# The small work of a state space group in three portions instead of seven

## The chip, the core and the metric

The kernel runs on one core of a Trainium2 chip. The metric is the device time of one execution in microseconds (us). A core has five engines that run side by side and wait for each other by semaphores: TensorE (PE, matrix products; the profile shows its weight loads apart, as PEld), VectorE (DVE), ScalarE (ACT), GpSimd (POOL) and SyncE (SP), which here issues the transfers between the chip's memory (HBM) and the core's own memory. Products are accumulated in eight PSUM banks of 128 x 512 floats.

## The reference, cut to what matters

One block of a hybrid model on 512 positions with width 1024: a norm, one wide projection, a state space branch and an attention branch that are gated and added, then a feed-forward part. Attention has nothing to do with the change except that its last step, the combination of three attention groups, runs on DVE at the same time. The state space branch is this:

```python
def ssd_chunked(xs, dt, A, Bm, Cm):
    ...                                   # G = 8 groups, K = 4 heads each, N = 128, Q = 128, 4 chunks
    X = (xs * dt[..., None]).reshape(b, c, Q, G, K, P)
    a_cs = jnp.cumsum(a, axis=-1)
    Ldec = jnp.exp(jnp.where(causal, seg, -jnp.inf))          # seg = a_cs_l - a_cs_s
    CB = jnp.einsum('bclgn,bcsgn->bcgls', Cc, Bc)
    y_diag = jnp.einsum('bcgkls,bcsgkp->bclgkp', CB[:, :, :, None] * Ldec, X)
    states = jnp.einsum('bclgn,bcgkl,bclgkp->bcgkpn', Bc, decay_states, X)
    ...                                   # prev: the states carried from chunk to chunk
    y_off = jnp.einsum('bclgn,bcgkpn,bcgkl->bclgkp', Cc, prev, jnp.exp(a_cs))
    return (y_diag + y_off).reshape(b, s, H, P)

def ssd_branch(z, xbc, dt_raw, conv_w, conv_b, dt_bias, a_log, d_skip, norm_g):
    xbc = jax.nn.silu(causal_dwconv(xbc, conv_w, conv_b))
    xs, Bm, Cm = jnp.split(xbc, (D_INNER, D_INNER + SSD_GROUPS * D_STATE), axis=-1)
    ...
    y = ssd_chunked(xs, dt, A, Bm, Cm) + d_skip.astype(f32)[:, None] * xs
    y = y.reshape(b, s, D_INNER) * jax.nn.silu(z.astype(f32))
    y = rms_norm(y.reshape(b, s, SSD_GROUPS, SSD_NORM_GROUP), norm_g.reshape(SSD_GROUPS, SSD_NORM_GROUP))
```

## The kernel before

**Pieces.** All weights come in pieces of 512 KB. SP loads a piece into `raw` (three buffers), ACT rounds it to `whi` (L103) and DVE subtracts to get the rest, `wlo` (L104); each of these has three buffers too, and one is free again when the last product that reads it is through. A channel piece is 24 products of 128 x 512 into one bank of four (tag "mm"): eight with whi and the high part of the activations (`hh,whi`), eight with the low part (`hl,whi`), eight with `hh,wlo` (`mm_chan`, L143).

**Ticks.** Small work hangs on this stream. It is written as generators; `tick()` lets each of them go on by one step when its wait, counted in ticks, is over. Ticks fall after product 12 of a piece, where `prefetch` also sets the next split going, and at the end of a piece. PE runs its instructions exactly in the order in which they are written, so a step's matmuls stand where its tick stands. For DVE, ACT, POOL and SP the scheduler chooses the order.

**A group of the state space stage** has six pieces: B and C (tile `bct`), two of xs (`xst`), two of z (`zs`). ACT and DVE run the convolution from PSUM (L676, L52), ACT the silu (L798). `ssd_side(g)` is the small work. `bc` holds the decays, copied to all partitions by SP (L688); DVE subtracts (L704), ACT takes relu (L706) and exp (L707). Then PE's portions, with the banks' tags:

- cb and bt (L713, L719): the products of C and B, and transposes of B, in the middle of a piece; DVE masks cb (L714) and multiplies it into bc (L722)
- xt, twice (L732): transposes of `xst`, at a piece's end and in the middle of the next; DVE makes `xdt` and `xdc` from each (L735, L738)
- st (L744): the chunk states from `xdc` and `btok`, in the two banks of tag "aux"; DVE carries them on as `prev` (L749 to L753)
- y with o (L763, L768), twice: y reads `bc` and `xdt`, o reads `bct` and `prev`; DVE and ACT go on from there (L771 to L774)
- n (L784): the norm's sum, from `sr` (ACT L780, POOL L777 and L781)

That is seven portions a group. [...] `load_decay(g + 2)` issues the next bc into the buffer that y1 has released. Two numbers set the waits between a group's portions for normal groups (`GN`), and others for the first two groups (`G0`, `G1`), the third (`G2W`), the norm (`NL`) and attention's combination (`COMB`), whose products and sums on DVE are L644, L646 and L652.

Of the kernel before, what the change touches and what calls it, by code (L numbers as in the profile page):

```python
# [16 lines left out]
P = 128  # L17
S = 512
NT = S // P
# [4 lines left out]

LAG, PVLAG = 2, 2
LAUNCH = (12, 5, 13)
COMB = 11
G0, G1, GN = (2, 1, 1, 1), (5, 2, 4, 2), (7, 2, 2)
G2W, YL = 4, 3
NL = (1, 3, 2, 1)  # L30

Z0, XS0, B0, C0, DT0 = 0, 2048, 4096, 5120, 6144
Q0, K0, V0, GS0, GA0 = 6176, 7712, 9248, 10784, 11808
# [5 lines left out]
def kernel(  # L39
# [6 lines left out]
    nc = tc.nc  # L46
# [648 lines left out]
    def ssd_side(g, bct, xst, zs, at):  # L695
        sp = late["b"]

        def T(tag, shape, bufs=1):
            return sp.tile(shape, F32, tag=tag, name=f"{tag}_{g}", bufs=bufs)

        hs = slice(4 * g, 4 * g + 4)
        mt, eb = decay[g]
        m4 = mt.rearrange("p h (c l) -> p h c l", c=NT)
        nc.vector.tensor_sub(m4, acs[:, :, hs].rearrange("p c h -> p h c").unsqueeze(3).broadcast_to((P, 4, NT, P)), m4)  # L704
        yield 1
        nc.scalar.activation(mt, mt, AF.Relu)  # L706
        nc.scalar.activation(mt, mt, AF.Exp, scale=-1.0)  # L707
        yield at["cb"]
        cbm = T("cbm", [P, NT, P])
        ps = bank("aux", f"ps_cb{g}")  # L710
        for c in range(NT):
            cs = slice(c * P, (c + 1) * P)
            nc.tensor.matmul(ps[:, cs], bct[:, 0, cs], bct[:, 1, cs], start=True, stop=True)  # L713
        nc.vector.tensor_mul(cbm, ps.rearrange("p (c l) -> p c l", c=NT),  # L714
                             triu.unsqueeze(1).broadcast_to((P, NT, P)))
        btok = T("btok", [P, 3, P])
        ps = bank("tr", f"ps_bt{g}")
        for c in range(3):
            nc.tensor.transpose(ps[:, c * P:(c + 1) * P], bct[:, 0, c * P:(c + 1) * P], ident)  # L719
        nc.scalar.copy(btok.rearrange("p c n -> p (c n)"), ps[:, :3 * P])  # L720
        yield 1
        nc.vector.tensor_mul(m4, m4, cbm.unsqueeze(1).broadcast_to((P, 4, NT, P)))  # L722
        yield at["x"]
        xdt = T("xdt", [P, NT, 4, 64])
        xdc = T("xdc", [P, 3, 4, 64])
        for hf in range(2):
            ps = bank("tr", f"ps_xt{g}_{hf}")
            for c in range(2):
                for j in range(2):
                    o = c * 256 + j * P  # L730
                    t0 = (2 * hf + c) * P
                    nc.tensor.transpose(ps[:, o:o + P], xst[:, j, t0:t0 + P], ident)  # L732
            p4 = ps.rearrange("p (c h d) -> p c h d", c=2, h=4)
            cc = slice(2 * hf, 2 * hf + 2)
            nc.vector.tensor_mul(xdt[:, cc], p4, dtt[:, cc, hs].unsqueeze(3).broadcast_to((P, 2, 4, 64)))  # L735
            n = 2 - hf
            cc = slice(2 * hf, 2 * hf + n)
            nc.vector.tensor_mul(xdc[:, cc], p4[:, :n], dtd[:, cc, hs].unsqueeze(3).broadcast_to((P, n, 4, 64)))  # L738
            yield 1
        prev = T("prev", [P, 3, 4, 64])  # L740
        pst = [bank("aux", f"ps_st{g}_{i}") for i in range(2)]
        sts = [pst[c // 2][:, c % 2 * 256:c % 2 * 256 + 256] for c in range(3)]
        for c in range(3):
            nc.tensor.matmul(sts[c], btok[:, c, :], xdc[:, c].rearrange("p h d -> p (h d)"),  # L744
                             start=True, stop=True)
        for c in range(3):
            p3 = sts[c].rearrange("p (h d) -> p h d", h=4)
            if c == 0:
                nc.vector.tensor_copy(prev[:, 0], p3)  # L749
            else:  # L750
                nc.vector.tensor_mul(prev[:, c], prev[:, c - 1],
                                     cdec[:, c, hs].unsqueeze(2).broadcast_to((P, 4, 64)))
                nc.vector.tensor_add(prev[:, c], prev[:, c], p3)  # L753
        yield at["y"]
        sq = T("sq", [P, 2, S])
        for j in range(2):
            b = 2 * g + j
            y = ysb[:, b, :]
            psy = bank("aux", f"ps_y{g}_{j}")
            for c in range(NT):  # L760
                cs = slice(c * P, (c + 1) * P)
                for i in range(2):
                    nc.tensor.matmul(psy[i * 64:(i + 1) * 64, cs], xdt[:, c, 2 * j + i, :],  # L763
                                     mt[:, 2 * j + i, cs], start=True, stop=True)
            pso = bank("aux", f"ps_o{g}_{j}")
            for c in range(1, NT):
                cs = slice(c * P, (c + 1) * P)
                nc.tensor.matmul(pso[:, cs], prev[:, c - 1, 2 * j:2 * j + 2, :].rearrange("p h d -> p (h d)"),  # L768
                                 bct[:, 1, cs], start=True, stop=True)
            stt(y, xst[:, j, :], dsk[:, b:b + 1], psy, ALU.mult, ALU.add)  # L770
            nc.vector.tensor_mul(sq[:, j, P:], pso[:, P:], eb[:, j, P:])  # L771
            nc.vector.tensor_add(y[:, P:], y[:, P:], sq[:, j, P:])
            nc.vector.tensor_mul(y, y, zs[:, j, :])
            nc.scalar.activation(sq[:, j, :], y, AF.Square)  # L774
            yield YL - j
        load_decay(g + 2)
        nc.gpsimd.tensor_add(sq[:, 0, :], sq[:, 0, :], sq[:, 1, :])  # L777
        yield NL[0]
        sr = sp.tile([P, 2, S], F32R, tag="sr", name=f"sr_{g}", bufs=1)
        nc.scalar.copy(sr[:, 0, :], sq[:, 0, :])  # L780
        nc.gpsimd.tensor_sub(sr[:, 1, :], sq[:, 0, :], sr[:, 0, :].bitcast(F32))  # L781
        yield NL[1]
        ps = bank("aux", f"ps_n{g}")
        nc.tensor.matmul(ps[0:1, :], ones_r, sr[:, 0, :], start=True, stop=False)  # L784
        nc.tensor.matmul(ps[0:1, :], ones_r, sr[:, 1, :], start=False, stop=True)
        vv = T("vv", [1, S])
        nc.scalar.activation(vv, ps[0:1, :], AF.Identity, bias=epsb[0:1], scale=1.0 / 256)
        nc.sync.dma_start(scr_v[g], vv)
        yield NL[2]
        rv = T("rv", [P, NT], 2)  # L790
        nc.sync.dma_start(rv, scr_v[g].rearrange("(p c) -> p c", c=NT))
        yield NL[3]
        nc.gpsimd.tensor_tensor(rv, rv, nhalf.broadcast_to((P, NT)), op=ALU.pow)
        nc.sync.dma_start(scr_r[g].rearrange("(p c) -> p c", c=NT), rv)
# [3 lines left out]
            nc.scalar.activation(o, o, AF.Silu)  # L798
        yield 1

    normal = dict(zip(("cb", "x", "y"), GN))
    tiles = {}

    def branch_tiles(g):
# [3 lines left out]
    for g in range(8):  # L808
        if g > 1:
            branch_tiles(g)  # L810
        if g > 1:
            start(ssd_side(g, *tiles[g], normal), G2W if g == 2 else 0)
        banks = []
        for i in range(6):
            w = next_piece()
            banks.append(bank("mm", f"ps_ssd{g}_{i}"))
            mm_chan(banks[i], w, hh, hl)
            if (g, i) == (0, 1):
                ab_cm.__exit__(None, None, None)
                late["a"] = sa_cm.__enter__()  # L820
                branch_tiles(0)
            if (g, i) != (0, 0):
                bct, xst, zs = tiles[g]
                for k in ((0, 1) if (g, i) == (0, 1) else (i,)):
                    if k < 2:
                        conv4(banks[k], 16 + 8 * k + g, bct[:, k, :])
                    elif k < 4:
                        conv4(banks[k], 2 * g + k - 2, xst[:, k - 2, :])
                    else:
                        nc.scalar.copy(zs[:, k - 4, :], banks[k])  # L830
            if i % 2 and g > 0:
                start(silus(tiles[g][i // 2]), 1)
            tick()
            if (g, i) == (0, 4):
                assert not any(s[0].__name__ in ("chain", "launch") for s in sides)
                aa_cm.__exit__(None, None, None)
                ap = ap_cm.__enter__()
                for k in "hl":
                    merged[k] = ap.tile([P, 4, S], F32R, tag="a" + k, name="a" + k)
                sb_cm = pool("ssd_b", side="right")  # L840
                late["b"] = sb_cm.__enter__()
                load_decay(0)
                load_decay(1)
                start(ssd_side(0, *tiles[0], dict(zip(("cb", "x", "y"), G0))), G0[3])
            if (g, i) == (0, 5):
                start(ssd_side(1, *branch_tiles(1), dict(zip(("cb", "x", "y"), G1))), G1[3])
                start(silus(*tiles[0]), 1)


# [261 lines left out]
```

## Time and profile before

| | |
|---|---|
| median of 3 runs | 1218.91 us (1218.9 to 1219.73) |
| profiled execution, its own time | 1220.35 us |
| its span in the profile | 1218.6 us |
| TensorE clock granted | 0.997 |
| PE busy | 1209.1 us, 99% |
| DVE busy | 685.6 us, 56% |
| ACT busy | 546.0 us, 45% |
| POOL busy | 79.7 us, 7% |
| matmuls of y / o / xt / st / cb / bt / n | 256 / 96 / 64 / 48 / 64 / 24 / 16 |

A timeline row gives start, duration, engine, line, operation, output<-inputs, partitions and shape, and how many instructions it joins. Matmuls overlap one another in the records (one product of 128 x 512 is shown with some 0.4 us but the next starts earlier), so costs on PE are read from starts. A PE that is busy is not always a PE that waits for nothing, so the list of waits is read beside it.

### The profile page before, as it was taken

What the parts mean: (1) busy time and instruction counts of PE and PEld (TensorE: products, weight loads), DVE (VectorE), ACT (ScalarE), POOL (GpSimd) and SP (SyncE); (2) the same over time, 40 slices, a digit from 0 to 9 for tenths busy, and PEclk for the clock granted to TensorE, in tenths of its full rate; (3) what the DMA queues carried; (4) which work ended last, traced back from release to release, by engine and by line L of the source; (5) the groups of instructions that cost most, each with busy time, mean ns of one, the idle gap of its engine ahead of it and who ended that gap; (6) DMA issues with size and microseconds to landing.
All of it is one profiled execution on the core that took longest, in us unless ns stands there. A gap on an engine that the chain in (4) does not pass through costs nothing.

```text
span 1218.6 us, 15107 instructions
## 1 busy us (share of the span) xinstructions
PE 1209.1 (99%) x5992; PEld 992.7 (81%) x5992; DVE 685.6 (56%) x908; ACT 546.0 (45%) x829; POOL 79.7 (7%) x57
## 2 busy tenths in 40 slices
PE   9999989999999999999999999999999999999998
PEld 7877767997888888888888888888888888888887
DVE  5214454447789987777744445645765665652322
ACT  4434446377746656456433323423544444441220
POOL 1021111100000101101011000000000000000000
PEclk9999989999999999999999999999999999999999
DMA  5444534422645544434325322252333333323230
GB/s 184 121 101 107 129 89 107 107 70 72 181 133 178 136 121 126 135 87 122 87 70 139 122 102 93 98 190 70 104 96 95 104 88 103 95 96 103 100 126 35
DMA packets 176056, 134.71 MB, mean 111 GB/s; under 512 B 12336, under 2 KB 150176, under 8 KB 174961
## 3 DMA queue, kind: packets, MB, share of 16 engines
q1 hardware_dynamic: 175985, 133.74, 38.7%
q8 instruction: 47, 0.77, 0.3%
q14 instruction: 24, 0.20, 0.1%
HBM read 131.12 MB, written 2.61 MB: 110 GB/s over the span
## 4 chain that ended last, share of the span: by engine, by line
PE 96%; DVE 1%; DMA 1%; POOL 1%; ACT 0%; issue 0%; SPq 0%; POOLq 0%; ACTq 0%; DVEq 0%
PE ps_ssd L143 22%; PE ps_u L143 20%; PE ps_wd L945 10%; PE ps_qk L143 10%; PE ps_gate L143 7%; PE ps_sp L918 7%; PE ps_v L407 6%; PE ps_wo L945 3%; PE ps_ap L143 2%; PE ps_y L763 1%; PE ps_pv L578 1%; PE ps_s L536 1%; PE ps_o L768 1%; PE ps_pt L567 1%; PE ps_st L744 1%; PE ps_xt L732 1%
## 5 line engine op out<-in xcount | busy, mean ns | idle before, releaser
L104 DVE TENSOR_TENSOR wlo<-raw,whi 128x1024 fp32r<-128x1024 f32 x194 | 244.6, 1262 | 366.9 <-ACT whi L103 203.6
L103 ACT CAST whi<-raw 128x1024 fp32r<-128x1024 f32 x194 | 203.5, 1049 | 324.4 <-PE ps_wd L945 79.8
L143 PE MATMUL ps_ssd<-hl,whi 128*128 128x512 f32 x384 | 102.9, 397 | 0.0
L143 PE MATMUL ps_ssd<-hh,whi 128*128 128x512 f32 x384 | 98.4, 398 | 0.0
L143 PE MATMUL ps_ssd<-hh,wlo 128*128 128x512 f32 x384 | 95.4, 390 | 0.0
L143 PE MATMUL ps_u<-h2h,whi 128*128 128x512 f32 (+1 forms) x368 | 87.9, 381 | 0.3 <-ACT h2h L220 0.2
L143 PE MATMUL ps_u<-h2l,whi 128*128 128x512 f32 (+1 forms) x368 | 87.5, 380 | 0.0
L143 PE MATMUL ps_u<-h2h,wlo 128*128 128x512 f32 (+1 forms) x368 | 87.4, 380 | 0.0
L143 PEld LDWEIGHTS ps_ssd<-hh,wlo 128*128 128x128 f32 x384 | 72.1, 188 | 15.9
L143 PEld LDWEIGHTS ps_ssd<-hh,whi 128*128 128x128 f32 x384 | 70.6, 188 | 14.0 <-issue 0.2
L143 PEld LDWEIGHTS ps_ssd<-hl,whi 128*128 128x128 f32 x384 | 70.2, 188 | 14.1 <-issue 0.2
L143 PEld LDWEIGHTS ps_u<-h2h,whi 128*128 128x128 f32 x368 | 67.2, 188 | 13.9 <-ACT h2h L220 0.8
L143 PEld LDWEIGHTS ps_u<-h2l,whi 128*128 128x128 f32 x368 | 67.2, 188 | 13.1
L143 PEld LDWEIGHTS ps_u<-h2h,wlo 128*128 128x128 f32 x368 | 67.2, 188 | 13.1
L52 DVE SCALAR_TENSOR_TENSOR facc<-ps_u,sc,facc 128x511 f32<-128x511 f32 x88 | 65.7, 746 | 5.8 <-ACT facc L1044 4.3
L555 ACT ACTIVATE s<-s,st 128x128 f32<-128x128 f32 (+1 forms) x96 | 39.8, 417 | 36.9 <-DVE st L549 20.5
L945 PE MATMUL ps_wd<-whi,actl 128*128 128x512 f32 x176 | 54.2, 389 | 0.0
L945 PE MATMUL ps_wd<-wlo,acth 128*128 128x512 f32 x176 | 54.2, 389 | 0.0
L945 PE MATMUL ps_wd<-whi,acth 128*128 128x512 f32 x176 | 54.1, 389 | 0.0
L143 PE MATMUL ps_qk<-hh,whi 128*128 128x512 f32 x192 | 51.0, 409 | 0.0
L143 PE MATMUL ps_qk<-hl,whi 128*128 128x512 f32 x192 | 47.9, 392 | 0.0
L143 PE MATMUL ps_qk<-hh,wlo 128*128 128x512 f32 x192 | 47.4, 389 | 0.0
(248 smaller groups left out, 1966.6 us busy)
## 6 DMA issues: line engine op xcount, KB each, us to landing
raw<-in_w_in_dram SPq DMA_DIRECT2D x100, 512.0 KB
raw<-in_w_up_dram SPq DMA_DIRECT2D x44, 512.0 KB
raw<-in_w_down_dram SPq DMA_DIRECT2D x22, 512.0 KB
bc<-scr_a SPq DMA_DIRECT2D x8, 1024.0 KB
raw<-in_w_ssd_proj_dram SPq DMA_DIRECT2D x16, 512.0 KB
hrb<-scr_q SPq DMA_DIRECT2D x12, 512.0 KB
eb<-scr_e SPq DMA_DIRECT2D x16, 256.0 KB
raw<-in_w_out_dram SPq DMA_DIRECT2D x8, 512.0 KB
```

Source lines behind the costliest of these rows:

```text
L52: nc.vector.scalar_tensor_tensor(o, a, s, b, op0=op0, op1=op1)
L103: nc.scalar.copy(hi, raw)
L104: nc.vector.tensor_sub(lo, raw, hi.bitcast(F32))
L143: nc.tensor.matmul(ps[:, t0:t0 + nt], a[:, k, c:c + n], b[:, k, t0:t0 + nt], start=(i == 0), stop=(i == total - 1))
L407: nc.tensor.matmul(pss[b], tok(g, kq * 2 + k, b, xx), w[:, k, :], start=(kq == 0 and j == 0 and k == 0), stop=(kq == 3 and j == 2 and k == 1))
L536: nc.tensor.matmul(pss[h][:, o:o + nk * P], qt[hp, j, q * P:(q + 1) * P], kt[hp, j, (q - nk + 1) * P:(q + 1) * P], start=True, stop=True)
L555: nc.scalar.activation(s[:, o:o + nk * P], s[:, o:o + nk * P], AF.Exp, bias=st[:, q, 0, 2 * j + h:2 * j + h + 1], accum_out=st[:, q, 1, 2 ...
L567: nc.tensor.transpose(pst[:, o:o + P], ss[h][:, o:o + P], ident)
L578: nc.tensor.matmul(pso[h * 64:(h + 1) * 64, q * P:(q + 1) * P], vt[:, q - nk + 1 + kb, (2 * j + h) * 64:(2 * j + h + 1) * 64], pts[h][:, o ...
L732: nc.tensor.transpose(ps[:, o:o + P], xst[:, j, t0:t0 + P], ident)
L918: nc.tensor.matmul(pss[j], w[:, k, cs], ys[k][xi], start=(k2 == 0 and i == 0 and k == 0), stop=(k2 == 7 and i == 2 and k == 1))
L945: nc.tensor.matmul(pss[b], xx[:, k0 + k, b * P:(b + 1) * P], ww[:, k, :], start=(k0 == 0 and j == 0 and k == 0), stop=(k0 == nk - 2 and j ...
```

## The change

A group now has three portions of its own, each at the end of a piece: A, with bt, both xt and cb; then st; then y0, o0, y1, o1. n joins a portion when it falls on the same tick. The second xt now uses a bank of tag "aux", y1, o1 and n use tag "tr"; xdc is computed ahead of xdt. The waits are renumbered, and `COMB` goes from 11 to 12. No instruction of PE, DVE or ACT is added or dropped except the order; line numbers of the changed kernel are one or two lower behind the top.

```diff
-COMB = 11
-G0, G1, GN = (2, 1, 1, 1), (5, 2, 4, 2), (7, 2, 2)
-G2W, YL = 4, 3
-NL = (1, 3, 2, 1)
+COMB = 12
+G0, G1, GN = (3, 2, 1), (8, 4, 2), (10, 4)
+NL = (2, 3, 2, 1)
...
-        yield at["cb"]
+        yield at["a"]
+        btok = T("btok", [P, 3, P])
+        ps = bank("tr", f"ps_bt{g}")
+        for c in range(3):
+            nc.tensor.transpose(ps[:, c * P:(c + 1) * P], bct[:, 0, c * P:(c + 1) * P], ident)
+        nc.scalar.copy(btok.rearrange("p c n -> p (c n)"), ps[:, :3 * P])
+        xdt = T("xdt", [P, NT, 4, 64])
+        xdc = T("xdc", [P, 3, 4, 64])
+        for hf in range(2):
+            ps = bank(("tr", "aux")[hf], f"ps_xt{g}_{hf}")
...
+            nc.vector.tensor_mul(xdc[:, cc], p4[:, :n], dtd[:, cc, hs].unsqueeze(3).broadcast_to((P, n, 4, 64)))
+            cc = slice(2 * hf, 2 * hf + 2)
+            nc.vector.tensor_mul(xdt[:, cc], p4, dtt[:, cc, hs].unsqueeze(3).broadcast_to((P, 2, 4, 64)))
         cbm = T("cbm", [P, NT, P])
         ps = bank("aux", f"ps_cb{g}")
...
         nc.vector.tensor_mul(cbm, ps.rearrange("p (c l) -> p c l", c=NT),
                              triu.unsqueeze(1).broadcast_to((P, NT, P)))
-        btok = T("btok", [P, 3, P])
...
         yield 1
         nc.vector.tensor_mul(m4, m4, cbm.unsqueeze(1).broadcast_to((P, 4, NT, P)))
-        yield at["x"]
...
+        yield 1
         prev = T("prev", [P, 3, 4, 64])
...
-            psy = bank("aux", f"ps_y{g}_{j}")
+            psy = bank(("aux", "tr")[j], f"ps_y{g}_{j}")
...
-            pso = bank("aux", f"ps_o{g}_{j}")
+            pso = bank(("aux", "tr")[j], f"ps_o{g}_{j}")
...
-            yield YL - j
+        yield 3
         load_decay(g + 2)
...
-        ps = bank("aux", f"ps_n{g}")
+        ps = bank("tr", f"ps_n{g}")
...
-            start(ssd_side(g, *tiles[g], normal), G2W if g == 2 else 0)
+            start(ssd_side(g, *tiles[g], normal))
```

How the order moves on the engines, at three places. A row gives line, operation, output<-inputs and shape; a number behind a name tells one buffer's use from another's.

DVE around group 0's y, before: `prev_2787` is the carried states of group 0, `ps_y_0_2815` its first y.

```order
L753 TENSOR_TENSOR prev_2787<-prev_2787,ps_st_0_2788 128x256
L751 TENSOR_TENSOR prev_2787<-prev_2787,cdec 128x256
L753 TENSOR_TENSOR prev_2787<-prev_2787,ps_st_1_2789 128x256
L104 TENSOR_TENSOR wlo_2849<-raw_2846,whi_2848 128x1024
L52 SCALAR_TENSOR_TENSOR xst_2622<-ps_ssd_3_2768,sc,xst_2622 128x511
L52 SCALAR_TENSOR_TENSOR ysb<-xst_2354,dsk,ps_y_0_2815 128x512
```

And in the changed kernel, `prev_2768` being the same states:

```order
L751 TENSOR_TENSOR prev_2768<-prev_2768,ps_st_0_2769 128x256
L103 TENSOR_TENSOR wlo_2795<-raw_2792,whi_2794 128x1024
L749 TENSOR_TENSOR prev_2768<-prev_2768,cdec 128x256
L103 TENSOR_TENSOR wlo_2867<-raw_2864,whi_2866 128x1024
L751 TENSOR_TENSOR prev_2768<-prev_2768,ps_st_1_2770 128x256
L51 SCALAR_TENSOR_TENSOR xst_2622<-ps_ssd_3_2779,sc,xst_2622 128x511
L51 SCALAR_TENSOR_TENSOR ysb<-xst_2354,dsk,ps_y_0_2815 128x512
```

The two splits (`wlo`) have moved in among the last steps of prev.

DVE in group 2, the changed kernel, the end of what stands between the convolution of piece 3 and the state portion (`xdc_3334` and `xdt_3333` are group 2's, `fb` belongs to attention's combination). From the first convolution step of `ps_ssd_3_3177` to the last row here there are 26 rows, 14 of them products and sums of the combination:

```order
L103 TENSOR_TENSOR wlo_3301<-raw_3298,whi_3300 128x1024
L643 TENSOR_TENSOR ysb<-ysb,fb_2_3226 128x512
L703 TENSOR_TENSOR bc_3250<-acs,bc_3250 128x2048
L645 TENSOR_TENSOR ysb<-ysb 128x512
L643 TENSOR_TENSOR ysb<-ysb,fb_0_3271 128x512
L643 TENSOR_TENSOR ysb<-ysb,fb_1_3276 128x512
L725 TENSOR_TENSOR xdc_3334<-ps_xt_0_3335,dtd 128x512
L651 TENSOR_TENSOR al<-ysb,ah 128x512
L643 TENSOR_TENSOR ysb<-ysb,fb_2_3281 128x512
L727 TENSOR_TENSOR xdt_3333<-ps_xt_0_3335,dtt 128x512
L725 TENSOR_TENSOR xdc_3334<-ps_xt_1_3342,dtd 128x256
L727 TENSOR_TENSOR xdt_3333<-ps_xt_1_3342,dtt 128x512
```

The last row frees the "aux" bank that st takes; in the kernel before, the combination's rows end ahead of the mask of cb and the first xt comes after them.

ACT in group 5, before (`xst_3972` is the group's xs, `bc_4203` the decays of the next group but one):

```order
L780 CAST sr_4236<-sq_4076 128x512
L720 COPY btok_4216<-ps_bt_4217 128x384
L706 ACTIVATE bc_4203<-bc_4203 128x2048
L103 CAST whi_4255<-raw_4253 128x1024
L798 ACTIVATE xst_3972<-xst_3972 128x1024
L830 COPY zs_3973<-ps_ssd_4_4184 128x512
L707 ACT_TABLE_LOAD
L707 ACTIVATE bc_4203<-bc_4203 128x2048
```

And now, with `xst_3978` for the same tile:

```order
L778 CAST sr_4242<-sq_4112 128x512
L705 ACTIVATE bc_4203<-bc_4203 128x2048
L102 CAST whi_4238<-raw_4236 128x1024
L706 ACT_TABLE_LOAD
L706 ACTIVATE bc_4203<-bc_4203 128x2048
L796 ACT_TABLE_LOAD
L796 ACTIVATE xst_3978<-xst_3978 128x1024
L828 COPY zs_3979<-ps_ssd_4_4184 128x512
```

The silu of xst, which the xt transposes read, stands behind relu, exp and both table loads; it stood between relu and the first table load.

More of the change, by code (lines that the diff above doesn't have):

```diff
@@ L707, in ssd_side @@
         nc.scalar.activation(mt, mt, AF.Exp, scale=-1.0)
-        yield at["cb"]
+        yield at["a"]
[8 more added lines that the diff above has]
+            ps = bank(("tr", "aux")[hf], f"ps_xt{g}_{hf}")
+            for c in range(2):
+                for j in range(2):
+                    o = c * 256 + j * P
+                    t0 = (2 * hf + c) * P
+                    nc.tensor.transpose(ps[:, o:o + P], xst[:, j, t0:t0 + P], ident)
+            p4 = ps.rearrange("p (c h d) -> p c h d", c=2, h=4)
+            n = 2 - hf
+            cc = slice(2 * hf, 2 * hf + n)
+            nc.vector.tensor_mul(xdc[:, cc], p4[:, :n], dtd[:, cc, hs].unsqueeze(3).broadcast_to((P, n, 4, 64)))
+            cc = slice(2 * hf, 2 * hf + 2)
+            nc.vector.tensor_mul(xdt[:, cc], p4, dtt[:, cc, hs].unsqueeze(3).broadcast_to((P, 2, 4, 64)))
         cbm = T("cbm", [P, NT, P])
@@ L715, in ssd_side @@
                              triu.unsqueeze(1).broadcast_to((P, NT, P)))
-        btok = T("btok", [P, 3, P])
[L717 to L720, printed above, removed]
         yield 1
         nc.vector.tensor_mul(m4, m4, cbm.unsqueeze(1).broadcast_to((P, 4, NT, P)))
-        yield at["x"]
[L724 to L739, printed above, removed]
+        yield 1
         prev = T("prev", [P, 3, 4, 64])
@@ L799, in silus @@
         yield 1
-    normal = dict(zip(("cb", "x", "y"), GN))
+    normal = dict(zip(("a", "y"), GN))
     tiles = {}
@@ L843 @@
                 load_decay(1)
-                start(ssd_side(0, *tiles[0], dict(zip(("cb", "x", "y"), G0))), G0[3])
+                start(ssd_side(0, *tiles[0], dict(zip(("a", "y"), G0))), G0[2])
             if (g, i) == (0, 5):
-                start(ssd_side(1, *branch_tiles(1), dict(zip(("cb", "x", "y"), G1))), G1[3])
+                start(ssd_side(1, *branch_tiles(1), dict(zip(("a", "y"), G1))), G1[2])
                 start(silus(*tiles[0]), 1)
```

## The prediction

> **What bounds the kernel now.** I read the page first, then what PE waited for, then PE's timeline over one steady state space group.
>
> ```profile
> PE 96%; DVE 1%; DMA 1%; POOL 1%; ACT 0%; issue 0%; SPq 0%; POOLq 0%; ACTq 0%; DVEq 0%
> ```
> ```profile
> PE ps_s L536 <- DVE s L543: 4.1, 1, 4.1
> ```
>
> The first line is the chain of work that ended last: PE carries 96% of it. The second is PE's longest wait, in attention, which the change does not touch; no wait of the state space stage is listed. So time can be won only where a portion makes PE's stream slower, and lost where a portion is reached before DVE or ACT has what it needs. Group 5, PE's rows (start, duration, what, count):
>
> ```profile
> 504.99 1.07 PE L143 MATMUL ps_ssd<-hl,whi 128*128 128x512 f32 x4
> 505.98 1.09 PE L763 MATMUL ps_y<-bc,xdt 128*64 128x128 f32 x16
> 507.01 0.94 PE L768 MATMUL ps_o<-bct,prev 128*128 128x128 f32 x6
> 507.70 1.17 PE L143 MATMUL ps_ssd<-hl,whi 128*128 128x512 f32 x4
> 508.71 2.00 PE L143 MATMUL ps_ssd<-hh,wlo 128*128 128x512 f32 x8
> ...
> 512.36 1.07 PE L143 MATMUL ps_ssd<-hl,whi 128*128 128x512 f32 x4
> 513.27 1.05 PE L713 MATMUL ps_cb<-bct 128*128 128x128 f32 x8
> 514.16 0.49 PE L719 MATMUL ps_bt<-ident,bct 128*128 128x128 f32 x3
> 514.40 1.17 PE L143 MATMUL ps_ssd<-hl,whi 128*128 128x512 f32 x4
> 515.42 1.99 PE L143 MATMUL ps_ssd<-hh,wlo 128*128 128x512 f32 x8
> ...
> 520.87 1.98 PE L143 MATMUL ps_ssd<-hh,wlo 128*128 128x512 f32 x8
> 522.68 0.60 PE L732 MATMUL ps_xt<-ident,xst 128*128 128x128 f32 x4
> 523.04 2.10 PE L143 MATMUL ps_ssd<-hh,whi 128*128 128x512 f32 x8
> 524.98 1.07 PE L143 MATMUL ps_ssd<-hl,whi 128*128 128x512 f32 x4
> ```
>
> Starts, not durations, add up. Eight products take 1.81 us (520.87 to 522.68), so a piece of 24 takes 5.44. A portion costs what it stretches the products around it by. cb with bt: 512.36 to 515.42 holds eight products, 3.06 − 1.81 = 1.25. The first xt: 520.87 to 524.98 holds sixteen, 4.11 − 3.62 = 0.49. n is two matmuls as wide as a product, so about 2 × 0.226 = 0.45. One y with its o: 504.99 to 508.71, 3.72 − 1.81 = 1.91.
>
> **The change, part by part: PE's stream.** The matmuls stay the same; fewer interruptions remain. What one is worth is what a portion costs beyond its own instructions. The eight cb start 0.111 us apart (513.27 to 514.16). At that pace four xt cost 0.44 of their 0.49, and cb with bt 1.22 of 1.25: entering and leaving costs 0.05 or less. In one portion, 19 × 0.111 + 0.05 = 2.16 against 1.25 + 2 × 0.49 = 2.23 now (the second xt at the first one's price): 0.07 saved, between 0 (if going from transposes to cb costs what going from products to y does: 504.99 to 505.98 for four products, 0.085 too much) and 0.12.
>
> For y the inner part is 505.98 to 507.70, 1.72 of the 1.91, so 0.19 surrounds it. Merged it is 2 × 1.72 + 0.19 and the change from o back to y, which no row shows: nothing at best, at worst the full 0.19 and half as much again (0.29, a loss of 0.1). I take 0.13 for it, nearer to the surround, since the kind of matmul does change there: 0.06 saved. n rides with st instead of xt: no difference. Costed at nothing are the other banks and xdc ahead of xdt: between two uses of a bank lies a piece of 5.44 us, in which DVE empties it in one operation of 0.7 (the xdt row below); without that cover each would cost up to 0.7. Together 0.13 a group, 1.0 us over eight; bounds 8 × (0 − 0.1) = −0.8 and 8 × (0.12 + 0.19) = 2.5.
>
> [...]
>
> **Group 0, y: the last prev is now late.** DVE and PE before:
>
> ```profile
> 342.95 0.42 DVE L753 TENSOR_TENSOR prev<-prev,ps_st 128x256 f32<-128x256 f32 x1
> 343.88 1.23 DVE L104 TENSOR_TENSOR wlo<-raw,whi 128x1024 fp32r<-128x1024 f32 x1 [0.50 <-PE ps_ssd L143]
> ```
> ```profile
> 343.71 1.09 PE L763 MATMUL ps_y<-bc,xdt 128*64 128x128 f32 x16
> 344.74 0.94 PE L768 MATMUL ps_o<-bct,prev 128*128 128x128 f32 x6
> ```
>
> prev is done at 343.37, before y starts; the split (wlo) waits for a buffer that the last products free, and runs 0.17 us into y. The change's DVE order puts that same split ahead of the last prev add. Then: y + 0.17, 1.23 for the split, 0.42 for the add = y + 1.82, while o is due at y + 1.03. Stall 0.8; not under 0.6, and up to 2.0 if another split is in the way.
>
> **Group 2, st: DVE behind.** st takes the banks of xt1 and cb, and xdc. Between the end of piece 3 and st the order gives DVE 14 products and sums of attention's combine, two al, three conv steps, two splits, the bc subtraction and four xdt/xdc. Prices:
>
> ```profile
> 401.55 2.31 DVE L104 TENSOR_TENSOR wlo<-raw,whi 128x1024 fp32r<-128x1024 f32 x1
> ...
> 417.84 0.68 DVE L735 TENSOR_TENSOR xdt<-ps_xt,dtt 128x512 f32<-128x512 f32 x1
> 418.44 0.73 DVE L52 SCALAR_TENSOR_TENSOR bct<-ps_ssd,sc,bct 128x509 f32<-128x509 f32 x1
> 419.10 0.41 DVE L738 TENSOR_TENSOR xdc<-ps_xt,dtd 128x256 f32<-128x256 f32 x1
> 419.43 1.21 DVE L104 TENSOR_TENSOR wlo<-raw,whi 128x1024 fp32r<-128x1024 f32 x1
> ```
>
> By starts a 128x512 operation is 0.60, a conv step 0.66, the short xdc 0.33; a split 1.21, the subtraction, four times as wide as a 0.60, about 2.3. 16 × 0.60 + 3 × 0.66 + 2 × 1.21 + 2.3 + 3 × 0.60 + 0.33 = 18.4, and 1.1 more for each split caught beside POOL, like the 2.31 above: 18.4 to 20.6. DVE starts on it 0.4 to 1.6 us after the last product of piece 3 begins (that product's end, then one or two operations of the portion still to do). PE reaches st after 72 products and the merged portion: 0.2 + 16.3 + 2.2 + n's 0.45 = 19.1. Stall between 0 (18.8 against 19.1) and 3.1; I take the middle, 1.5.
>
> **Groups 4 to 6, xt0: silu late.** The transposes read silu(xst). ACT runs it before the table load and exp in the trace; the change's order puts it behind relu, split, table load, exp and a second table load. Prices from the rows of POOL, the DMA view of 507 to 512.5, and the rows of SP, DVE and ACT:
>
> ```profile
> 510.67 1.29 POOL L777 TENSOR_TENSOR sq<-sq 128x512 f32<-128x512 f32 x1 [18.39 <-ACT sq L774]
> ```
> ```profile
> DMA packets 879, 1.65 MB, mean 299 GB/s; under 512 B 43, under 2 KB 598, under 8 KB 751
> ```
> ```profile
> 507.12 0.34 SPq L688 DMA_DIRECT2D bc<-scr_a  x1
> ```
> ```profile
> 513.63 2.70 DVE L704 TENSOR_TENSOR bc<-acs,bc 128x2048 f32<-128x2048 f32 x1
> ```
> ```profile
> 511.99 0.62 ACT L780 CAST sr<-sq 128x512 fp32r<-128x512 f32 x1 [0.47 <-POOL sq L777]
> ...
> 516.36 1.92 ACT L706 ACTIVATE bc<-bc 128x2048 f32<-128x2048 f32 x1 [1.20 <-DVE bc L704]
> 518.18 1.04 ACT L103 CAST whi<-raw 128x1024 fp32r<-128x1024 f32 x1
> 519.12 1.06 ACT L798 ACTIVATE xst<-xst 128x1024 f32<-128x1024 f32 x1
> ...
> 520.66 1.28 ACT L707 ACT_TABLE_LOAD   x1
> 521.95 1.92 ACT L707 ACTIVATE bc<-bc 128x2048 f32<-128x2048 f32 x1
> ```
>
> Silu ended at 520.18, 2.5 us ahead of xt at 522.68. In the change the chain starts at the end of y1, which frees bc's buffer. The transfer takes at most 6.5 (507.12 until the subtraction at 513.63, though DVE's steps lay between) and at least 3.5 (1.0 MB at the rate of the line above); I take 4.6. Then the subtraction, 2.3 when nothing stretches it; POOL's sum 1.29, which waits for DVE to let go; sr 0.62, which stands ahead of relu on ACT; relu 1.92, split 1.04, load 1.28, exp 1.92, load 1.28, silu 1.06: 17.3, and 16.2 to 19.2 by the transfer's bounds. PE gets from y1's end to xt0 in the last o (0.7), three pieces (16.3) and three transposes (0.3): 17.3. So −1.1 to 1.9 late; the time cannot be won below zero, so the middle of a tie costs something: I take 0.3 for each of three groups, 0.9. SP issues bc and its two small companions some 0.7 us earlier in the group than now (the end of piece 2 plus a merged portion of 3.0, against half a piece and one y, 3.7), ahead of the same weight loads; PE never waited for a weight in this stage, and this moves none of them by more than that. Group 7 has no such bc, and in group 3 ACT's order keeps silu ahead of exp.
>
> **Sum.** −1.0 + 0.8 + 1.5 + 0.9 = +2.2 us. The profiled execution took 1220.35, its span 1218.6, so 1.7 lie around the span; it is 1.4 above the median of 1218.91. Its span becomes 1220.8. From the median the change gives 1221.1 us, 0.18% more.
>
> **Rivals.**
>
> *Stalls at their upper ends (slower).* One mechanism: ACT's row with exp and two table loads ahead of silu. If the bc transfer loses to the weight loads queued beside it, each of groups 4 to 6 waits up to 1.9, 5.7 us instead of 0.9: 1218.91 − 1.0 + 0.8 + 1.5 + 5.7 = 1225.9, and at two thirds of that 1224.0, which I give as its time. It decides from 0.4 us per group, where the sum passes 0.2%. For it: the row at 513.63 shows the subtraction itself stretched to 2.70. Against: the tie of 17.3 and 17.3.
>
> *No stall (no measurable change, or barely faster).* DVE and ACT catch up; then only PE's saving is left: 1217.9, or 1216.4 at its bound of 2.5. For it: both engines do idle in these stretches, ACT 1.20 us ahead of the relu row. Against: the prev add and silu are late because of what the order puts ahead of them, not because of load.
>
> *Each interruption costs more than the rows show (faster).* If leaving the product stream stops PE, and part of what I put on a portion's own matmuls is that stop, four interruptions fewer a group at the 0.19 that surrounds y save 0.76 a group, 6.1 us: 1212.8 without stalls, 1216.0 with the 3.2 above. For it: the 0.19. Against: cb with bt shows only 0.03.
>
> **Chances.** The forecast 0.50, of which 0.10 lies over the bound of no change; more stalls 0.25; no stall 0.13, of which 0.03 is faster; costly interruptions 0.12. Within 0.2% of 1218.91 (2.44 us, about what a measurement of this kernel can tell from no change): 0.40 + 0.10 = 0.50; slower 0.10 + 0.25 = 0.35; faster 0.15. The likeliest case's own range is 1219.0 to 1222.5. The range that holds 8 of 10 reaches up past the first rival's time and down past no stall, to where the stalls meet the costly interruptions: 1216.4 to 1224.6.
>
> **What would show it.** PE's waits after: ps_o on DVE's prev once, about 0.8; ps_st once in group 2, about 1.5; ps_xt on ACT's xst three times, 0.3 each. PE's starts across the merged A portion 2.16 beyond the products' pace, across the merged y 3.76. Wrong would be: a listed wait at another place, a merged y at 3.4 or below, or no wait at all.

## The result, and the profile after

The changed kernel took 1227.81 us in the median of 4 runs (1226.55 to 1229.84) against 1219.32 for the kernel before (the 1218.91 given ahead of the prediction was the median of three runs; a fourth took 1222.17); the ratio is 1.0062, with a 95% interval of 1.005 to 1.0074. It is slower, and outside the range that was given. The profiled execution took 1226.9 us with a span of 1225.2, which is 6.6 more than the span before.

What PE waited for in the changed kernel (total, times, longest):

```profile
PE ps_s L535 <- DVE s L542: 4.3, 1, 4.3
PE ps_st L742 <- DVE xdt L727: 3.1, 1, 3.1
PE ps_xt L721 <- ACT xst L796: 2.3, 3, 0.8
PE ps_warma L232 <- DVE ones L153: 1.1, 1, 1.1
PE ps_o L766 <- DVE prev L751: 0.8, 1, 0.8
```

The first and the fourth were there before. The other three are new, and they stand where the prediction put them: st in group 2, xt in groups 4 to 6, o in group 0. They make 6.2 us, where 3.2 was forecast.

PE's rows from group 2's state portion on, and below them the same place of group 5 in the kernel before, where nothing waits:

```profile
410.74 2.88 PE L742 MATMUL ps_st<-xdc,btok 128*128 128x256 f32 x6 [3.07 <-DVE xdt L727]
413.07 2.73 PE L142 MATMUL ps_ssd<-hh,whi 128*128 128x512 f32 x8
415.63 1.99 PE L142 MATMUL ps_ssd<-hl,whi 128*128 128x512 f32 x8
```
```profile
529.55 1.46 PE L744 MATMUL ps_st<-xdc,btok 128*128 128x256 f32 x6
530.66 2.19 PE L143 MATMUL ps_ssd<-hh,whi 128*128 128x512 f32 x8
532.69 1.98 PE L143 MATMUL ps_ssd<-hl,whi 128*128 128x512 f32 x8
```

The wait is not the whole cost. From st's start to the next product 2.33 us go by instead of 1.11, and the eight products behind it take 2.56 instead of 2.03: 1.75 us more, after the wait has ended. Windows of one us each over that stretch say why. The columns are the window, its length, busy time of PE, PE's loads, DVE, ACT and POOL, then the clock granted to PE, the share of DMA and GB/s:

```profile
410.00:411.00 1.00, 0.26 (x1) 0.29 (x2) 1.00 (x2) 1.00 (x2) 0.00 (x0) 0.88 0.04 10
411.00:412.00 1.00, 1.00 (x3) 0.82 (x3) 1.00 (x2) 1.00 (x3) 0.00 (x0) 0.50 0.00 0
412.00:413.00 1.00, 1.00 (x4) 0.73 (x4) 1.00 (x3) 1.00 (x3) 0.00 (x0) 0.50 0.00 0
```

PE stood still until 410.74, and then worked at half clock for 3.4 us: the 0.88 of the first window puts its start at 410.76, and the window from 414, with 0.91, its end at 414.18. At 0.50 that is 1.7 us of work lost, which is the 1.75. This state portion with its n stretches the products by 6.77 us, against 1.78 in groups 3 to 7: 4.99 us for a wait that the list shows with 3.1. The last 0.16 of it is a matter of counting: the list starts the wait where n's record ends (407.67), but the next start was due at 407.51.

DVE, which was late there: the first convolution step of piece 3, and the last step that st waits for.

```profile
391.09 0.75 DVE L51 SCALAR_TENSOR_TENSOR xst<-ps_ssd,sc,xst 128x511 f32<-128x511 f32 x1
...
409.92 0.68 DVE L727 TENSOR_TENSOR xdt<-ps_xt,dtt 128x512 f32<-128x512 f32 x1
```

That is 19.5 us of work without a gap, within the 18.4 to 20.6 that was reckoned. (The stretch beside POOL, whose rows run from 391.99 to 393.59 and from 394.32 to 395.61, fell on two rows of the combination, 1.13 and 1.45 us instead of 0.68, and not on the splits, 1.21 each.) But it began at 391.09, and the last product of piece 3 at 388.35 (piece 4's row starts at 388.57): 2.7 us, not 0.4 to 1.6. In between DVE ran five operations: three steps of group 1's second y and, among them, an al (L651) and a product of the combination (L643).

Group 5's late silu, by the rows of SP, DVE, ACT and PE of the changed kernel:

```profile
509.48 0.34 SPq L687 DMA_DIRECT2D bc<-scr_a  x1
```
```profile
515.19 2.29 DVE L703 TENSOR_TENSOR bc<-acs,bc 128x2048 f32<-128x2048 f32 x1 [0.61 <-DMA bc<-scr_a]
```
```profile
518.67 0.62 ACT L778 CAST sr<-sq 128x512 fp32r<-128x512 f32 x1 [2.10 <-POOL sq L775]
519.20 1.92 ACT L705 ACTIVATE bc<-bc 128x2048 f32<-128x2048 f32 x1
521.02 1.03 ACT L102 CAST whi<-raw 128x1024 fp32r<-128x1024 f32 x1
522.07 1.28 ACT L706 ACT_TABLE_LOAD   x1
523.36 1.92 ACT L706 ACTIVATE bc<-bc 128x2048 f32<-128x2048 f32 x1
525.30 1.28 ACT L796 ACT_TABLE_LOAD   x1
526.59 1.06 ACT L796 ACTIVATE xst<-xst 128x1024 f32<-128x1024 f32 x1
```
```profile
526.48 0.49 PE L711 MATMUL ps_bt<-ident,bct 128*128 128x128 f32 x3
527.70 1.09 PE L721 MATMUL ps_xt<-ident,xst 128*128 128x128 f32 x8 [0.73 <-ACT xst L796]
```

An ACT_TABLE_LOAD of 1.28 us stands ahead of this exp and another behind it, ahead of silu; where silu and exp follow one another on ACT, the kernel before has such a row too. The chain is the predicted one, link by link; the first link is longer. The subtraction began 5.7 us after the issue (6.7 in group 4, 5.8 in group 6), where 4.6 was taken, and it was waiting for the transfer. The three merged portions cost 0.92, 0.93 and 1.04 us more than the 2.15 of a group without a wait.

### The profile page after: what moved, and what is told of

It reads as the page before. It is cut to its first block, busy times and chain, and to the rows that moved or that the text cites. A ratio compares the mean times of both kernels' runs of the same rounds, so it can differ in the third digit from the quotient of the medians.

```text
span 1225.2 us, 15103 instructions
## 1 busy us (share of the span) xinstructions
PE 1209.4 (99%) x5992; PEld 994.6 (81%) x5992; DVE 681.5 (56%) x908; ACT 544.7 (44%) x829; POOL 81.3 (7%) x57
## 4 chain that ended last, share of the span: by engine, by line
PE 89%; DVE 3%; DMA 2%; ACT 2%; issue 2%; POOL 1%; SPq 0%; POOLq 0%; DVEq 0%; ACTq 0%
PE ps_u L142 20%; PE ps_ssd L142 15%; PE ps_wd L943 10%; PE ps_qk L142 10%; PE ps_gate L142 7%; PE ps_sp L916 7%; PE ps_v L406 5%; PE ps_wo L943 4%; PE ps_ap L142 2%; PE ps_pv L577 1%; PE ps_s L535 1%; PE ps_pt L566 1%; PE ps_y L761 1%; PE ps_o L766 1%; PE ps_st L742 1%
## 5 line engine op out<-in xcount | busy, mean ns | idle before, releaser
L103 DVE TENSOR_TENSOR wlo<-raw,whi 128x1024 fp32r<-128x1024 f32 x194 | 241.1, 1244 | 390.4 <-ACT whi L102 220.8
L142 PE MATMUL ps_ssd<-hl,whi 128*128 128x512 f32 x384 | 96.0, 390 | 0.0
```

Of the source, the lines that this page charges most:

```text
L103: nc.vector.tensor_sub(lo, raw, hi.bitcast(F32))
L142: nc.tensor.matmul(ps[:, t0:t0 + nt], a[:, k, c:c + n], b[:, k, t0:t0 + nt], start=(i == 0), stop=(i == total - 1))
```

## The experiments

**Group 0's y later.**

```diff
-G0, G1, GN = (3, 2, 1), (8, 4, 2), (10, 4)
+G0, G1, GN = (3, 4, 1), (8, 4, 2), (10, 4)
```

> Group 0's y portion comes two ticks later (the middle number of G0 goes from 2 to 4). Theory (the three late suppliers are the whole loss, and they add up): PE's wait of 0.8 us at ps_o on DVE's prev is gone, the waits at ps_st (3.1) and ps_xt (2.3 in all) stay, the time falls by 0.8 us. Rival (DVE as a whole is too slow, a wait that is taken away comes back behind): the sum of PE's waits in the state space stage stays at 6.2 us, within 0.3, and so does the time.

Measured: 1224.39 us, ratio to the kernel before 1.0034 (1.002 to 1.0047). PE's waits:

```profile
PE ps_xt L721 <- ACT xst L796: 2.5, 3, 1.0
PE ps_st L742 <- DVE xdt L727: 1.8, 1, 1.8
PE ps_warma L232 <- DVE ones L153: 1.1, 1, 1.1
PE ps_o L766 <- ACT vv L785: 0.9, 1, 0.9
```

The wait on prev is gone, but neither theory has it right. The second o of group 1 now waits 0.9 for ACT to empty n's bank, since n has come into the same portion and both use the banks of tag tr: a wait of the same size in another place. And st waits only 1.8, after which the stretch shows no half clock (3.80 us against 1.78, so 2.0 for the wait of 1.8). More was won than 0.8, and by group 2, not by group 0. PE stood 0.95 us at that o, right ahead of piece 3, and DVE then began on st's work 1.4 us after the last product of that piece began, not 2.7; so a part of st's wait has only moved forward.

**The combination earlier.**

```diff
-COMB = 12
+COMB = 9
```

> Attention's combination starts three ticks earlier (COMB 9 instead of 12); the portions stay as the change has them. Theory: DVE has done the combination's products before group 2's xdt, the wait of 3.1 us at ps_st is gone, and with it the stretch of half clock behind it, about 1.9 us more: 5.0 us faster than the changed kernel, granted clock back at 0.997. Rival (DVE has too much to do in this stage, wherever the combination lies): a wait of 2 us or more turns up at another portion of groups 1 to 3, and less than 2 us are won.

Measured: 1225.63 us, 1.0055 (1.0035 to 1.0076), spread widely (1222.28 to 1234.79). PE's waits:

```profile
PE ps_xt L721 <- ACT xst L796: 5.9, 4, 2.7
...
PE ps_xt L721 <- DVE ft L626: 0.9, 1, 0.9
```

st's wait and its half clock are gone (no ps_st in the list; 0.999 of the clock was granted over the execution, 0.996 in the changed kernel), as the theory said; the time was not won, as the rival said. But of the new waits only the 0.9 us on ft, in group 1, are DVE's. The larger ones are at silu: xt in group 4 went from 0.7 to 2.7, and in group 3 a wait of 1.4 is new. There ACT's order differs from that of the changed kernel: silu ran at 440.57, behind exp and a second table load, where the changed kernel runs it ahead of them. In group 4 the bc transfer was issued at 464.74, and the subtraction that waited for it began at 473.34, 8.6 us later, against 6.7 in the changed kernel. Why that transfer took longer still was not settled; in the run with 13 more products below it took 8.3 in the same place.

**The other y portions earlier.**

```diff
-G0, G1, GN = (3, 2, 1), (8, 4, 2), (10, 4)
+G0, G1, GN = (3, 2, 1), (8, 4, 2), (10, 3)
```

> The y portion of groups 2 to 7 comes one tick earlier, in the middle of a piece instead of at its end (GN = (10, 3)). The chain from the end of y1 over bc's transfer, subtraction, relu, exp and two table loads to silu(xst) then starts 2.7 us earlier, the next xt0 is due at the same time. Theory: the three waits at ps_xt (0.73 to 0.8 each; 2.9 us by the stretch of the portions) are gone, st and o of groups 2 and 0 wait as before: 2.9 us faster than the changed kernel. Rival (silu is late because ACT is full, not because of that chain): the waits stay above 0.5 us each.

Measured: 1224.23 us, 1.0031 (1.0019 to 1.0044); a second time 1224.9, 1.0034. The span is 2.6 shorter than that of the changed kernel, where 2.9 was expected. The waits of the first:

```profile
PE ps_st L742 <- DVE xdt L727: 2.6, 1, 2.6
PE ps_warma L232 <- DVE ones L153: 1.1, 1, 1.1
PE ps_o L766 <- DVE prev L751: 0.8, 1, 0.8
```

All three waits at xt are gone and nothing has come in their place. Relu, exp and both table loads still run ahead of silu on ACT (a convolution step of 0.77 stands among them where a split of 1.03 stood), so it was enough that bc's buffer came free 2.7 us earlier. The rival, a full ACT, is out.

**PE kept busy while it would wait.** Two runs, on the changed kernel and on the one with the earlier y; the products add work and take none away.

```diff
+        if g == 2:
+            idle = bank("mm", "ps_idle")
+            for k in range(13):
+                nc.tensor.matmul(idle, hh[:, k % 8, :P], hh[:, k % 8, :], start=(k == 0), stop=(k == 12))
         prev = T("prev", [P, 3, 4, 64])
```

> In group 2, between n and st, 13 more products of 128 x 512 are put on PE, 2.95 us of work into a bank that nothing reads; DVE's and ACT's work is unchanged. Theory (the stop of 3.1 us makes the clock drop to half for the 3.2 us behind it): st starts when it did, the clock stays at 1.00, st and the products behind it run at their usual pace, and the kernel is 1.9 us faster with more work on PE. Rival (st and the products behind it are slow because they wait for DVE's mask and split): no faster, the stretch behind st stays 1.9 us too long.

Measured: 1226.72 us, 1.0055 (1.0037 to 1.0073), not to be told from the changed kernel. In the profiled execution, at 1229.94 the slowest of the four, the clock behind st stayed at 1.00 and st took 1.19 us to the next product, the eight behind it 2.04, as the theory says. DVE's mask of cb and its split start 0.2 us ahead of st and 0.4 behind it, just as in the changed kernel, and nothing is slow beside them: that is against the rival. But st came later, since DVE had waited 0.7 us longer for the combination's data, so that PE still stood 1.78 us ahead of it, and in group 4 PE waited 2.73 us for silu, with half clock behind that wait (0.50 from 488 to 490). The case was too noisy to give a price, so it was repeated where the waits at xt are gone.

> The same kernel as y_earlier, taken again as the measure for the next one on the same chip: one stop of 2.6 us at ps_st in group 2, half clock for some 3.3 us behind it.

> As y_early_again with 11 more products in group 2 between n and st (2.5 us of work into a bank that nothing reads). Theory (the clock drops because PE stands still): st starts within 0.3 us of when it did, the clock stays at 1.00 there, and the kernel is 1.6 to 2.0 us faster, with more work: of the 4.54 us by which n with st is stretched, the wait stays and the part behind it goes. Rival (DVE's mask and split hold up st and the products behind it): no faster, and the products behind st keep the gaps of 0.4 to 0.8 us.

Measured: 1224.9 us without (1.0034, 1.002 to 1.0047) and 1223.35 with the 11 products (1.0024, 1.0013 to 1.0036). Without them PE stood 3.08 us at st, not the 2.63 of the first time:

```profile
411.59 2.61 PE L742 MATMUL ps_st<-xdc,btok 128*128 128x256 f32 x6 [3.08 <-DVE xdt L727]
413.64 2.98 PE L142 MATMUL ps_ssd<-hh,whi 128*128 128x512 f32 x8
416.46 1.98 PE L142 MATMUL ps_ssd<-hl,whi 128*128 128x512 f32 x8
```

The stretch of n and st in group 2 is 6.76 us without and 4.31 with them, the added 2.5 us of work included. But 0.74 of these 2.45 us are not the products' doing: attention, where nothing differs, took that much longer with them, so PE came to n that much later, and DVE did not. The medians lie 1.55 apart and the spans 1.7; the intervals overlap, so the trace carries this more than the times. One window and PE's rows with the products:

```profile
412.00:413.00 1.00, 1.00 (x6) 0.87 (x6) 1.00 (x2) 1.00 (x2) 0.00 (x0) 1.00 0.00 0
```
```profile
409.10 2.68 PE L741 MATMUL ps_idle<-hh 128*128 128x512 f32 x11
411.62 1.46 PE L746 MATMUL ps_st<-xdc,btok 128*128 128x256 f32 x6
412.72 2.19 PE L142 MATMUL ps_ssd<-hh,whi 128*128 128x512 f32 x8
414.75 1.98 PE L142 MATMUL ps_ssd<-hl,whi 128*128 128x512 f32 x8
```

The clock stays at 1.00, st takes 1.10 and the eight products 2.03, as where nothing waits. From st's start to the second eight products 3.13 us go by, and 4.87 without the added ones: 1.74, the same price of the half clock as in the changed kernel. So the slow rows behind this stop came from the stop itself and not from DVE.

**All waits taken away.**

```diff
-COMB = 12
-G0, G1, GN = (3, 2, 1), (8, 4, 2), (10, 4)
+COMB = 8
+G0, G1, GN = (3, 3, 1), (8, 4, 2), (10, 3)
```

> The three portions stay as the change has them (y, o, y, o in one), and only the numbers of the waits differ: the combination four ticks earlier (COMB 8), group 0's y one tick later (G0 = (3, 3, 1)), the other y one tick earlier (GN = (10, 3)). Theory (the change is a small gain on PE, and its loss is the late suppliers alone): no wait of PE above 0.3 us in the state space stage, clock 1.00 there, merged portions at 2.13 to 2.15 and 3.79 us, and a time 1.2 us under the kernel before, since a group's portions go from 2.22 + 3.86 + 1.81 to 2.14 + 3.79 + 1.78. Rival (the suppliers have no slack left, a wait only moves): waits of 2 us or more in all stay in the stage and the time stays above the kernel before.

Measured: 1218.7 us, 0.9983 (0.9973 to 0.9994), faster than the kernel before. The waits above 0.3 us are attention's and the start's alone:

```profile
PE ps_s L535 <- DVE s L542: 5.0, 1, 5.0
PE ps_warma L232 <- DVE ones L153: 1.1, 1, 1.1
```

The merged portions cost 2.13 to 2.15 and 3.79 us in every group; n stands with st in group 2 alone. From the first product on xs, B and C (`ps_ssd`) to the first of the next matrix but one (`ps_ap`) 424.3 us go by, and 425.9 in the kernel before: 1.5 less, where 1.2 was expected.

The three portions of themselves are a gain. What the changed kernel lost, it lost by waits that other numbers avoid. Whether other numbers would help the kernel before too was not tried.

**Both y, then both o.**

```diff
         for j in range(2):
-            b = 2 * g + j
-            y = ysb[:, b, :]
             psy = bank(("aux", "tr")[j], f"ps_y{g}_{j}")
+            banks2.append(psy)
...
+        for j in range(2):
+            b = 2 * g + j
+            y = ysb[:, b, :]
+            psy = banks2[j]
             pso = bank(("aux", "tr")[j], f"ps_o{g}_{j}")
```

> As waits_gone, and within the merged portion PE runs y0, y1, o0, o1 instead of y0, o0, y1, o1. Theory (each change between the 64-column y and the other kinds costs about 0.1 to 0.2 us, as the 0.202 and 0.214 at y to o and the 0.205 at o to y in the changed kernel's starts against a pace of 0.11 show): the portion goes from 3.79 to 3.51, 8 times 0.28, so 2.2 us faster than waits_gone. Rival (those starts are only uneven, the matmuls catch up): the same 3.79 and no difference in time.

Measured: 1216.23 us, 0.9962 (0.9949 to 0.9975), the fastest of all. The portion in group 5:

```profile
537.48 1.07 PE L142 MATMUL ps_ssd<-hl,whi 128*128 128x512 f32 x4
538.48 1.97 PE L761 MATMUL ps_y<-bc,xdt 128*64 128x128 f32 x32
540.38 1.60 PE L770 MATMUL ps_o<-bct,prev 128*128 128x128 f32 x12
541.74 1.17 PE L142 MATMUL ps_ssd<-hl,whi 128*128 128x512 f32 x4
542.75 1.53 PE L142 MATMUL ps_ssd<-hh,wlo 128*128 128x512 f32 x6
```

The same 44 matmuls cost 3.47 us instead of 3.79, 0.33 for two changes of kind fewer, 2.6 over eight groups; the medians lie 2.5 apart, and from `ps_ssd` to `ps_ap` it is 2.7 less. So a change between y and o cost about 0.16 here, an estimate from the 0.33 for two.

**One part of the change alone.** The kernel before, with only y and o merged and in the better order:

```diff
-G0, G1, GN = (2, 1, 1, 1), (5, 2, 4, 2), (7, 2, 2)
+G0, G1, GN = (2, 1, 1, 1), (5, 2, 6, 2), (7, 2, 2)
...
-            psy = bank("aux", f"ps_y{g}_{j}")
+            psy = bank(("aux", "tr")[j], f"ps_y{g}_{j}")
+            banks2.append(psy)
...
-            yield YL - j
+        yield YL
...
-        ps = bank("aux", f"ps_n{g}")
+        ps = bank("tr", f"ps_n{g}")
```

> The kernel before with one part of the change only: y and o of a group in one portion at the end of a piece, in the order y0, y1, o0, o1, with the second pair and n in banks of tag tr; cb, bt and the two xt stay where they were. Theory (the loss comes from the later xt, silu and xdt, not from the merged y): no new wait above 0.3 us, 8 times 3.86 - 3.51 = 2.8 us faster than the kernel before. Rival (merging y itself makes bc's transfer or prev late): a wait at ps_xt or ps_o of 0.5 us or more, and no gain.

Measured: 1221.66 us, 1.0011 (1.0001 to 1.002): no gain, as the rival said, although each y portion costs the 3.47 us: 8 times 0.39 are 3.1 us of gain, and the new waits make 3.1 us.

```profile
PE ps_st L744 <- DVE xdc L738: 1.6, 2, 1.2
PE ps_xt L732 <- ACT xst L802: 1.5, 1, 1.5
```

They are st in group 2 and xt in group 4, two of the changed kernel's places, though xt, cb and bt stand where they did before. In group 4 the subtraction waited for bc (until 467.04), ACT started the convolution of the second xs piece behind exp (476.24), and silu waited for DVE to end it. To merge y alone moves enough of DVE's and ACT's work to make them late.

## Why the prediction was wrong

- **PE's own gain: right.** Forecast was 0.07 a group for the merged A and 0.06 for the merged y. The portions went from 2.22 to 2.13 to 2.15, and from 3.86 to 3.79. n with st gave 0.03 more where n had stood alone. A steady group takes 0.16 less; over eight groups that is 1.3 us, forecast 1.0.
- **Group 0, the late prev: right.** 0.8 forecast, 0.8 listed, 0.83 by the stretch of the portion.
- **Group 2, st: the place and the cause right, the size wrong.** 1.5 was forecast and 4.99 came. Two steps failed. "DVE starts on it 0.4 to 1.6 us after the last product of piece 3 begins" was 2.7: I counted one or two of the y portion's steps still to do, and there were three, with two rows of the combination among them. That makes the wait 3.07, the upper end of the bound. And the sum took a stop of PE at its own length. A further 1.75 us came from the half clock behind it, for which the sum had no term.
- **Groups 4 to 6, xt: the place and the chain right, the size wrong.** "I take 4.6" for bc's transfer was 5.7 to 6.7. With that added, 17.3 becomes 18.4 or more against 17.3, and 2.9 us came instead of 0.9. "The middle of a tie" was too kind to the change. POOL's sum, which was put at 1.29 behind the subtraction, took 2.93 and 2.71 beside it in groups 5 and 6; in group 4 it began 0.5 ahead of the subtraction and took 1.29, and the subtraction took 2.94 instead of 2.29.
- **The rivals.** The first had the sign, and 1224.0; it put the excess on the three waits at xt alone, which gave half of the 5.7 at its upper end, and did not have the clock. No stall is what the kernel with other numbers shows, at 0.9983. Costly interruptions are out for going into and out of the product stream, 0.03 to 0.08 us here, but right between y and o, about 0.16, where the change keeps them.
- **The account.** 0.83 + 4.99 + 2.90 − 1.3 is 7.4; the kernel before had 0.3 of its own at group 2's st, so 7.1. PE's starts in the stage move by 7.0. Attention, which is not changed, took 0.4 less in this execution, and 6.6 is the difference of the spans. Why the medians lie further apart, 8.5, was not pursued; the changed kernel's runs spread over 3.3 us.

## What to carry to other kernels

With PE's stream full, as here at 99%, fewer interruptions were worth only what surrounds a portion, 0.03 to 0.08 us for each merging; what decided was whether each input was there at the new place, so reckon the supplier's chain to that place from the first transfer on, and count a tie as a loss. Look in the trace for what the clock does behind a stop before a stop is priced at its length. And where kinds of matmul alternate, sort them: the order y, y, o, o was worth more than all merging (2.6 us against 1.3).

## What the runs showed of the hardware

**A stop of 3.07 us cost 1.75 us more than itself.** The kernel before shows a half clock too, and the prediction overlooked it: at the end of attention's wait of 4.1 us (until 156.08) the clock goes to 0.50.

```profile
152.00:156.00 4.00, 0.01 (x1) 0.00 (x0) 4.00 (x7) 0.00 (x0) 0.00 (x0) 0.97 0.23 39
156.00:160.00 4.00, 3.92 (x11) 2.70 (x12) 1.98 (x7) 3.27 (x10) 0.00 (x0) 0.50 0.41 120
```

In the state space stage the waits of 3.07 us (changed kernel), 3.08 and 2.63 us (the earlier y, twice) were followed by 3.4 us at 0.50. Two of 1.8 were not: with 13 more products all windows from 410 to 416 show 1.00, and with group 0's y later the stretch of 3.80 against 1.78 leaves no room for it. Of two waits of 2.73 us one was, with 0.94, 0.50 and 0.70 in the windows of 2 us from 486 to 492 (group 4 with 13 more products, the first row), and one was not, with 1.00 in each us from 484 to 488 (group 4 with the combination earlier, the second):

```profile
487.46 1.71 PE L721 MATMUL ps_xt<-ident,xst 128*128 128x128 f32 x8 [2.73 <-ACT xst L800]
484.97 1.09 PE L721 MATMUL ps_xt<-ident,xst 128*128 128x128 f32 x8 [2.73 <-ACT xst L796]
```

So the length of the wait alone did not decide it; what did was not shown.

**A merged portion can be hurt by a bank.** n and the second o share two banks of one tag. When they came into one portion, in group 1 with group 0's y later, o waited 0.95 us for ACT to empty n's bank.
